# Two small moves in a planned schedule: a pair of VectorE transposes goes behind 35 filler units, and the bonus product changes its PSUM pool

## The chip, the core and the metric

The kernel runs on one core of one Trainium2 chip. The metric is device time in microseconds (us) of one execution, the median of several. Besides the times there is a profile of one further execution.

## The reference, cut to what matters

A decoder trunk of two layers works on 512 positions of width 1024 in float32. Each layer has three token mixers side by side (RWKV-7, retention, a spatial gating unit), gates that merge them, and a gated MLP. The change lies in the RWKV-7 mixer alone:

```python
def step(state, inp):
    r_t, w_t, k_t, v_t, kk_t, a_t = inp
    sa = jnp.einsum('bhvk,bhk->bhv', state, -kk_t)
    state = (state * w_t[:, :, None, :]
             + sa[..., None] * (kk_t * a_t)[:, :, None, :]
             + v_t[..., None] * k_t[:, :, None, :])
    y = jnp.einsum('bhvk,bhk->bhv', state, r_t)
    return state, y
...
y = y + jnp.sum(r * k * r_k, axis=-1, keepdims=True) * v
```

The last line is the bonus: for each head of 64 columns, the sum of r·k·r_k, times v.

## The kernel before, in words

**Order of the work.** Nearly all large products are float32 products made of three passes (`mm3`, lines 152 to 162): activations and weights are split into a high part and a low part, and line 156 issues three matmuls of 512 columns for each pair. Weights come in units of 128 rows by 512 columns. A unit is loaded by SyncE's queue (line 126), its high part is made by ScalarE (the cast of line 139, tiles `wh` or `sh`), its low part by VectorE (the subtraction of line 140, tiles `wl` or `sl`). One unit feeds 12 matmuls. `unit()` (lines 94 to 114) prepares units ahead of their use; in the stage of the change `AHEAD[None]` is 2, so that the call that hands out unit n has just emitted lines 139 and 140 of unit n + 2. The tags `wh` and `wl` have three buffers each.

**Who orders it.** Instructions are emitted in the order of the Python program. A scheduler then orders each engine's queue, by the order of emission, priorities and a simulated timeline; each engine works its queue off in order. `keep_in_program_order` (called `po`) fixes one instruction behind the instruction emitted just before it on the same engine; it adds no wait for another engine.

**RWKV-7 in chunks.** For each of four pairs of heads, `prep(m)` (lines 526 to 581) makes the decays and the scaled keys, and, in eight chunks of 64 positions, the products that the recurrence needs (lines 571 and 574), which ScalarE copies out of PSUM (lines 575 and 576). `bonus(m)` (lines 583 to 591) multiplies r·k·r_k by a block matrix of ones (lines 588 and 589), and VectorE multiplies the result by v (line 590). PSUM has eight banks: four of tag `acc`, taken by `acc()`, for the long accumulations of line 156, and four of tag `sm`, taken by `sm()`, for short products. `prep` takes six `sm` banks one after the other, and `bonus` takes a seventh.

**Solve.** Within a chunk a unit triangular system of 64 rows must be inverted for each head. `solve` (lines 756 to 821) inverts the blocks of 32 rows on VectorE, by a forward substitution of 31 dependent steps (lines 785 to 790), and joins the blocks on TensorE (lines 808 and 817). Between the two stand the first pair of 32 by 32 transposes, which makes `TD` (line 794), the second pair, which makes `TT` (line 797), and `diag(TT)`, four copies of diagonal blocks from `TT` into `G` (two on ScalarE, line 769, two on GpSimd, line 771). `then()` emits the turning of the scaled keys (lines 629 to 635): a VectorE transpose (line 631), a transfer out and eight transfers back on SyncE's queue. Line 808 reads `TD` and blocks of `G` that `diag` doesn't write; line 817 reads `TT`; the recurrence's loop (line 664) reads the diagonal blocks.

**Filler.** While VectorE substitutes, TensorE works on gate projections: `self.fill(n)` emits n steps of a generator, each one unit (`gates`, lines 433 to 448). Two steps make one accumulator, which VectorE takes out of PSUM (line 443). `FILL = (36, 2, 1)`: 36 steps go before line 808 is reached, two before line 817, one at each pause of the loop. In the profile's names `hi`, `lo` are the parts of the activations.

Of the kernel before, what the change touches and what calls it, by code (L numbers as in the profile page):

```python
# [23 lines left out]
FILL = (36, 2, 1)  # L24
# [27 lines left out]
class Emit:  # L52
# [408 lines left out]
    def rwkv(self, l, nst):  # L461
        nc, V, A, a = self.nc, self.nc.vector, self.nc.scalar, self.a
# [4 lines left out]
        po = self.tc.keep_in_program_order if l == 0 else lambda i: i  # L467
# [49 lines left out]
        hv, po = [slice(0, 64), slice(64, 128)], self.tc.keep_in_program_order  # L517
# [65 lines left out]
        def bonus(m):  # L583
            kp, r, v = kc[m], rc[m], Vf[m]
            V.scalar_tensor_tensor(kp, r, self.p("rk", m), kp, op0=MUL, op1=MUL)
            kh, kl = self.split(kp, self.r)
            pbn = self.sm()
            po(T.matmul(pbn, self.bonesR, kl, start=True, stop=False))
            po(T.matmul(pbn, self.bonesR, kh, start=False, stop=True))
            V.tensor_tensor(kp, v, pbn, op=MUL)  # L590
            bv.append(kp)
# [9 lines left out]
        prep(0)  # L601
        cols3(2)
        bonus(0)
        prep(1)
        cols3(3)
        bonus(1)
        prep(2)
        gd = col(13)
        bonus(2)
        prep(3)  # L610
        bonus(3)
# [144 lines left out]
    def solve(self, G, n2, then):  # L756


        V, A, T = self.nc.vector, self.nc.scalar, self.nc.tensor
        flat = lambda t: t.rearrange("p t s -> p (t s)")  # L760
        po = self.tc.keep_in_program_order
        grp = [slice(32 * i, 32 * i + 32) for i in range(4)]
        def diag(d):

            for i, R in enumerate(grp):
                g = G[R, :, 32 * (i % 2):32 * (i % 2) + 32]
                o, s = (d[R], g) if d is GD else (g, d[R])
                if i < 2:
                    A.copy(o, s)
                else:  # L770
                    self.nc.gpsimd.tensor_copy(o, s)
        GD = self.rw((128, 32, 32), "cs", 3)
        diag(GD)
        for h in range(2):
            self.nc.gpsimd.memset(G[64 * h + 32:64 * h + 64, :, 0:32], 0.0)
        NS = self.rw((128, 32, 32), "cs", 3)
        TS = self.rw((128, 32, 32), "cs", 3)
        TMP = self.rwp.tile([128, 288], F32, name=self.nm("TMP"))
        V.memset(TS, 0.0)
        V.memset(flat(TS)[:, 0:1024:33], 1.0)  # L780
        V.transpose(NS, GD.rearrange("p u t -> p t u"))
        nu = TMP[:, 256:288]
        V.transpose(nu, n2)
        V.tensor_tensor(NS, NS, nu.unsqueeze(1).to_broadcast([128, 32, 32]), op=MUL)
        for k in range(31):
            r, c = 31 - k, k + 1
            tmp = TMP[:, :r * c].rearrange("p (r c) -> p r c", c=c)
            V.tensor_tensor(tmp, NS[:, k + 1:, k:k + 1].to_broadcast([128, r, c]),
                            TS[:, k:k + 1, :c].to_broadcast([128, r, c]), op=MUL)
            V.tensor_tensor(TS[:, k + 1:, :c], TS[:, k + 1:, :c], tmp, op=ADD)  # L790
        V.tensor_tensor(TS, TS, nu.unsqueeze(2).to_broadcast([128, 32, 32]), op=MUL)
        TD = self.rw((128, 32, 32), "cs", 3)
        for e in (slice(0, 16), slice(16, 32)):
            V.transpose(TD[:, :, e].rearrange("p u s -> p s u"), TS[:, :, e].rearrange("p t s -> p s t"))
        TT = self.rw((128, 32, 32), "cs", 3)
        for e in (slice(0, 16), slice(16, 32)):
            V.transpose(TT[:, :, e].rearrange("p u t -> p t u"), TS[:, e])
        diag(TT)
        then()
        lo = [slice(64 * h, 64 * h + 32) for h in range(2)]  # L800
        hi = [slice(64 * h + 32, 64 * h + 64) for h in range(2)]
        self.fill(FILL[0])

        zs = [self.r((128, 16, 32), n="zs") for _ in range(2)]
        z = [[self.sm((128, 16, 32)) for _ in range(2)] for _ in range(2)]
        for g, i in [(g, i) for g in range(2) for i in range(16)]:
            for h in range(2):
                po(T.matmul(z[g][h][(hi, lo)[i % 2][h], i, :], G[lo[h], 16 * g + i, 32:64], TD[lo[h], 16 * g + i, :], start=True, stop=True))
        for g in range(2):
            for h in range(2):  # L810
                for e in range(2):
                    (V.tensor_copy if h else A.copy)(zs[g][hi[h], e::2], z[g][h][(hi, lo)[e][h], e::2])
        self.fill(FILL[1], True)
        pt = [[self.sm((128, 16, 32)) for _ in range(2)] for _ in range(2)]
        for g, i in [(g, i) for g in range(2) for i in range(16)]:
            for h in range(2):
                po(T.matmul(pt[g][h][(lo, hi)[i % 2][h], i, :], zs[g][hi[h], i, :], TT[hi[h], 16 * g + i, :], start=True, stop=True))
        for g in range(2):
            for h in range(2):
                for e in range(2):  # L820
                    (V.tensor_copy if h else A.copy)(G[lo[h], 16 * g + e:16 * g + 16:2, 32:64], pt[g][h][(lo, hi)[e][h], e::2])
# [620 lines left out]
```

## Time and profile before

| what | us |
|---|---|
| median of 3 runs | 1702.07 (1701.75 to 1702.5) |
| the profiled execution's own time | 1702.98 |
| its span | 1701.0 |
| TensorE busy | 1687.0 (99%) |
| VectorE busy | 1217.3 (72%) |
| ScalarE busy | 795.6 (47%) |
| GpSimd busy | 240.7 (14%) |

Layer 0's `solve` reaches line 808 at 200.9 us of the span, layer 1's at 1047.8 us. In a row of the timeline the first number is the start, the second the length, both in us; then come the engine (PE for TensorE, DVE for VectorE, ACT for ScalarE, POOL for GpSimd, SPq for SyncE's queue), the line, the operation, the tile written and the tiles read. A bracket at the end tells how long the engine stood idle before, and whose end released it.

### The profile page before, as it was taken

To read this page: it belongs to the slowest core of one execution; us is meant where nothing else is said; L and a number is where in the kernel's file an instruction comes from. 1 tells how busy PE (TensorE), PEld (TensorE's weight loads), DVE (VectorE), ACT (ScalarE), POOL (GpSimd) and SP (SyncE) were. 2 spreads that over 40 slices of the span, in tenths; PEclk is the share of its full clock that TensorE was granted. 3 is DMA by queue.
4 is the path that set the end of the run, shared out by engine and by line. 5 is a ranking of instruction groups with operands and counts; after the bars stand their busy time and mean duration, and the time that the engine had idled before them with its cause. 6 is when DMAs were issued, how large, how long until landed. Compare 5 with 4: busy or idle time off the path is not lost.

```text
span 1701.0 us, 27848 instructions
## 1 busy us (share of the span) xinstructions
PE 1687.0 (99%) x10214; PEld 1379.5 (81%) x10214; DVE 1217.3 (72%) x2113; ACT 795.6 (47%) x1367; POOL 240.7 (14%) x336
## 2 busy tenths in 40 slices
PE   9999999999999999999999999999999999999998
PEld 7888777888888888888888888777888888888886
DVE  6887745578669877655568887455786688887776
ACT  6563433554345444433346544435542544444565
POOL 2121000003301200003321210000132012220000
PEclk9999999999999999999999999999999999999999
DMA  5336553524544533147743265535254534443775
GB/s 179 90 106 196 176 179 103 174 93 161 192 144 147 193 124 99 63 143 264 242 150 97 93 206 182 178 101 180 87 163 166 153 96 142 143 141 115 244 242 168
DMA packets 147768, 260.01 MB, mean 153 GB/s; under 512 B 19600, under 2 KB 39952, under 8 KB 147632
## 3 DMA queue, kind: packets, MB, share of 16 engines
q1 hardware_dynamic: 122960, 192.87, 36.5%
q0 software_dynamic: 15888, 49.95, 8.8%
q10 hardware_dynamic: 8784, 15.42, 2.5%
q8 instruction: 80, 1.31, 0.3%
q14 instruction: 56, 0.46, 0.1%
HBM read 212.94 MB, written 45.22 MB: 152 GB/s over the span
## 4 chain that ended last, share of the span: by engine, by line
PE 90%; DMA 4%; DVE 3%; ACT 1%; issue 1%; SPq 1%; POOL 0%; ACTq 0%; DVEq 0%; POOLq 0%
PE acc L156 81%; PE sm L156 3%; PE sm L664 2%; DMA wr<-wall 2%; PE sm L917 1%; DVE wl L140 1%; PE sm L571 1%; DMA tr<-qkt 1%; DVE sl L140 0%; ACT wh L139 0%; PE sm L1022 0%; SPq L230 0%; ACT sh L139 0%; DMA x<-xT 0%; DMA bkS<-tr 0%
## 5 line engine op out<-in xcount | busy, mean ns | idle before, releaser
L156 PE MATMUL acc<-hi,sh 128*128 128x512 f32 x1108 | 431.9, 390 | 0.0
L156 PE MATMUL acc<-lo,sh 128*128 128x512 f32 x1108 | 431.6, 390 | 0.0
L156 PE MATMUL acc<-hi,sl 128*128 128x512 f32 x1108 | 424.5, 390 | 0.0
L139 ACT CAST sh<-wr 128x512 fp32r<-128x512 f32 (+1 forms) x375 | 226.7, 614 | 305.5 <-PE acc L156 166.9
L140 DVE TENSOR_TENSOR sl<-wr,sh 128x512 fp32r<-128x512 f32 (+1 forms) x375 | 253.5, 683 | 106.2 <-ACT sh L139 79.3
L140 DVE TENSOR_TENSOR wl<-wr,wh 128x512 fp32r<-128x512 f32 x238 | 168.5, 710 | 145.3 <-ACT wh L139 142.3
L139 ACT CAST wh<-wr 128x512 fp32r<-128x512 f32 x238 | 146.6, 619 | 241.2 <-PE acc L156 151.9
L156 PEld LDWEIGHTS acc<-lo,sh 128*128 128x128 f32 x1108 | 208.1, 188 | 43.8 <-issue 0.9
L156 PEld LDWEIGHTS acc<-hi,sl 128*128 128x128 f32 x1108 | 208.0, 188 | 43.5 <-DVE gth L1037 0.3
L156 PEld LDWEIGHTS acc<-hi,sh 128*128 128x128 f32 x1108 | 208.0, 188 | 43.3 <-issue 0.3
L156 PE MATMUL acc<-lo,wh 128*128 128x512 f32 x588 | 232.1, 395 | 1.5 <-DVE lo L215 1.1
L156 PE MATMUL acc<-hi,wl 128*128 128x512 f32 x588 | 230.3, 392 | 0.8 <-DVE wl L140 0.7
L156 PE MATMUL acc<-hi,wh 128*128 128x512 f32 x588 | 229.2, 390 | 0.0
L1088 ACT ACTIVATE cv<-fu,pc 128x512 f32<-128x512 f32 x88 | 71.7, 816 | 138.7 <-DVE fu L1086 138.6
L156 PEld LDWEIGHTS acc<-hi,wl 128*128 128x128 f32 x588 | 110.4, 188 | 27.2 <-DVE wl L140 3.4
L156 PEld LDWEIGHTS acc<-lo,wh 128*128 128x128 f32 x588 | 110.4, 188 | 26.7 <-DVE lo L215 1.8
L156 PEld LDWEIGHTS acc<-hi,wh 128*128 128x128 f32 x588 | 110.4, 188 | 22.1 <-issue 0.2
L156 PE MATMUL acc<-ah,sh 128*128 128x512 f32 x352 | 108.4, 389 | 0.0
L1089 DVE SCALAR_TENSOR_TENSOR cv<-fu,pc,cv 128x511 f32<-128x511 f32 x88 | 65.8, 749 | 34.5 <-ACT cv L1088 34.5
L156 PE MATMUL acc<-wl,hi 128*128 128x512 f32 x212 | 86.1, 406 | 0.0
L1086 DVE TENSOR_TENSOR fu<-acc,rsF 128x512 f32<-128x512 f32 x88 | 60.3, 685 | 31.9 <-PE acc L156 31.0
L156 PE MATMUL acc<-wh,hi 128*128 128x512 f32 x212 | 82.8, 391 | 0.0
(358 smaller groups left out, 2413.8 us busy)
## 6 DMA issues: line engine op xcount, KB each, us to landing
wr<-wall SPq DMA_DIRECT2D x488, 256.0 KB, 2.8
gd<-gth ACTq DMA_DIRECT2D x48, 256.0 KB, 3.2
gth<-gd POOLq DMA_DIRECT2D x48, 256.0 KB, 3.4
pre<-wdt POOLq DMA_DIRECT2D x44, 256.0 KB, 5.7
ts<-pre POOLq DMA_DIRECT2D x44, 256.0 KB, 2.8
wr<-ts SPq DMA_DIRECT2D x44, 256.0 KB, 3.9
wr<-wdn SPq DMA_DIRECT2D x40, 256.0 KB, 4.0
wr<-wdt SPq DMA_DIRECT2D x33, 256.0 KB, 3.6
```

The costliest lines, as they stand in the source:

```text
L139: self.kept(self.nc.scalar.copy(hi[:, :n], raw[:, :n]))
L140: self.kept(self.nc.vector.tensor_tensor(lo[:, :n], raw[:, :n], hi[:, :n], op=SUB))
L156: i = self.nc.tensor.matmul(*x, **y, **kw)
L571: i = T.matmul(pK[hv[1 - h], j, :], bk[hv[h], c, 1, :], x[hv[h], c, :], start=True, stop=True)
L664: po(T.matmul(o, l, r, start=start, stop=True, skip_group_check=True))
L917: po(T.matmul(X[h][:, i, :], lhsT, rhs, start=new[h], stop=stop, skip_group_check=True))
L1086: V.tensor_tensor(u, ps, self.rsF, op=MUL)
L1088: A.activation(t, u, AF.Identity, scale=self.p("cw2", j), bias=self.p("cb", j))
L1089: V.scalar_tensor_tensor(t[:, 1:], u[:, :511], self.p("cw1", j), t[:, 1:], op0=MUL, op1=ADD)
```

## The change

The second pair of transposes and `diag(TT)` are emitted behind 35 of the 36 filler steps, and each of the two transposes is kept behind what was emitted before it on VectorE. `then()` is now emitted ahead of them. The bonus product's bank comes from the four `acc` banks. No operation is added or taken away.

```diff
@@ -584,7 +584,7 @@
             kh, kl = self.split(kp, self.r)
-            pbn = self.sm()
+            pbn = self.acc()
             po(T.matmul(pbn, self.bonesR, kl, start=True, stop=False))
             po(T.matmul(pbn, self.bonesR, kh, start=False, stop=True))
             V.tensor_tensor(kp, v, pbn, op=MUL)
@@ -792,14 +792,15 @@
         TD = self.rw((128, 32, 32), "cs", 3)
         for e in (slice(0, 16), slice(16, 32)):
             V.transpose(TD[:, :, e].rearrange("p u s -> p s u"), TS[:, :, e].rearrange("p t s -> p s t"))
-        TT = self.rw((128, 32, 32), "cs", 3)
-        for e in (slice(0, 16), slice(16, 32)):
-            V.transpose(TT[:, :, e].rearrange("p u t -> p t u"), TS[:, e])
-        diag(TT)
         then()
         lo = [slice(64 * h, 64 * h + 32) for h in range(2)]
         hi = [slice(64 * h + 32, 64 * h + 64) for h in range(2)]
-        self.fill(FILL[0])
+        self.fill(FILL[0] - 1)
+        TT = self.rw((128, 32, 32), "cs", 3)
+        for e in (slice(0, 16), slice(16, 32)):
+            po(V.transpose(TT[:, :, e].rearrange("p u t -> p t u"), TS[:, e]))
+        diag(TT)
+        self.fill(1)
```

## The prediction

> **What bounds the kernel now.** I read the page first, then the list of who waits for whom with TensorE (PE) as the waiting engine, then the timeline of the stretches that this list points to.
>
> ```profile
> span 1701.0 us, 27848 instructions
> PE 1687.0 (99%) x10214; PEld 1379.5 (81%) x10214; DVE 1217.3 (72%) x2113; ACT 795.6 (47%) x1367; POOL 240.7 (14%) x336
> PE 90%; DMA 4%; DVE 3%; ACT 1%; issue 1%; SPq 1%; POOL 0%; ACTq 0%; DVEq 0%; POOLq 0%
> ```
>
> ```profile
> PE acc L156 <- DVE sl L140: 2.0, 6, 0.5
> PE acc L334 <- DVE rst L331: 1.5, 1, 1.5
> PE acc L156 <- DVE lo L215: 1.1, 2, 0.7
> PE acc L156 <- DVE wl L140: 0.7, 1, 0.7
> PE sm L664 <- DVE s L724: 0.4, 2, 0.2
> PE sm L588 <- ACT Y L576: 0.4, 1, 0.4
> PE acc L156 <- ACT wh L139: 0.3, 1, 0.3
> ```
>
> PE is busy for 99% of the span and makes 90% of the chain that ended last. The change removes no matmul, so only PE's pauses can shrink. All that the list names is 6.4 us. Two of its rows are what the change touches: 0.7 us, once, for a weight's low part from VectorE (line 140), and 0.4 us, once, for the bank of the bonus product (line 588, released by ScalarE's copy of line 576). No row shows PE waiting for an `acc` bank to be emptied (lines 443, 493). A fifth of a per cent of the time, about what a measurement of this kernel can tell from no change, is 3.4 us, over half of the list. The gain to be had is thus small from the outset.
>
> **The moved transposes, layer 0.** The first rows are PE's, then VectorE's and ScalarE's.
>
> ```profile
> 165.80 0.39 PE L156 MATMUL acc<-lo,wh 128*128 128x512 f32 x1
> 168.29 0.39 PE L156 MATMUL acc<-hi,wl 128*128 128x512 f32 x1
> ...
> 191.36 0.39 PE L156 MATMUL acc<-lo,wh 128*128 128x512 f32 x1
> 192.72 0.50 PE L156 MATMUL acc<-hi,wl 128*128 128x512 f32 x1 [0.74 <-DVE wl L140]
> 195.71 0.50 PE L156 MATMUL acc<-hi,wl 128*128 128x512 f32 x1
> 198.11 0.39 PE L156 MATMUL acc<-lo,wh 128*128 128x512 f32 x1
> ```
>
> ```profile
> 187.97 2.26 DVE L794 STREAM_TRANSPOSE cs<-cs 128x512 f32<-128x512 f32 x2
> 190.10 2.04 DVE L797 STREAM_TRANSPOSE cs<-cs 128x512 f32<-128x512 f32 x2
> 191.99 0.68 DVE L140 TENSOR_TENSOR wl<-wr,wh 128x512 fp32r<-128x512 f32 x1
> 194.96 0.69 DVE L140 TENSOR_TENSOR wl<-wr,wh 128x512 fp32r<-128x512 f32 x1 [1.70 <-ACT wh L139]
> 197.78 0.68 DVE L140 TENSOR_TENSOR wl<-wr,wh 128x512 fp32r<-128x512 f32 x1
> ```
>
> ```profile
> 188.58 0.63 ACT L139 CAST wh<-wr 128x512 fp32r<-128x512 f32 x1 [0.46 <-PE acc L156]
> 192.18 2.10 ACT L769 COPY GB<-cs 32x1024 f32<-32x1024 f32 x2 [2.97 <-DVE cs L797]
> 194.31 0.62 ACT L139 CAST wh<-wr 128x512 fp32r<-128x512 f32 x1
> ```
>
> The first two PE rows are the first and the last of a unit's 12 matmuls: 11 steps in 2.49 us, 0.226 us each. The unit that begins at 191.36 is the 34th filler unit. Its high part was ready at 189.2 (cast 188.58 + 0.63); its low part could have followed at 190.1, but stood in VectorE's queue behind the second pair of transposes until 191.99. PE waits. The pair does more: ScalarE, done with that cast at 189.2, has the `diag` copies next in its queue, stands idle 2.97 us until the pair is done, copies for 2.10 us, and only then casts the 35th unit (194.31), whose low part comes late as well (PE at 195.71). From 191.36 to 198.11 PE issues two units, 24 matmuls, in 6.75 us; at 0.226 they need 5.43. The pair costs 1.3 us here.
>
> Behind the change the pair stands behind line 140 of the 37th unit (the 35th call prepares two ahead), before the row at 197.78, the third line 140 behind the one at 191.99. That one needs the 34th unit's buffers, free at about 194.5 without the pause (191.36 + 12 x 0.226 + 0.39); cast and subtraction add 0.62 and 0.69, so the pair runs at about 196 to 198. VectorE waits for nothing new: line 794, at 187.97, comes behind the whole substitution. Queued behind the pair are line 140 of the 38th unit and line 443 of the 18th gate; behind ScalarE's copies, now at about 198 to 200.1, the casts of the 38th and 39th. Who waits for these:
>
> ```profile
> L808 PE MATMUL sm<-cs,GB x128: 191/191/212, 200.9 to 202.1; 32*32 32x32 f32 x128
> L817 PE MATMUL sm<-cs,zs x256: 184/191/212, 207.9 to 1056.0; 32*32 32x32 f32 x128
> 202.19 0.50 PE L156 MATMUL acc<-lo,wh 128*128 128x512 f32 x1
> ```
>
> The 37th unit starts at 202.19, the 38th a unit later at 204.9, and `TT` is first read at 207.9; with 1.3 us gained, 203.6 and 206.6. A line 140 that the pair holds until 198 is done by 198.7, and one whose cast waits for the copies until 200.1 by 201.4: 2 us early at the least. `diag` writes other blocks of `G` than line 808 reads, so line 808 doesn't wait for the copies. I take the whole 1.3 us as gained; the ends are a loss of 1.3 (the same pause at the new place, and in layer 1 as well) and a gain of 1.3.
>
> **The moved transposes, layer 1.**
>
> ```profile
> 1042.64 2.06 DVE L797 STREAM_TRANSPOSE cs<-cs 128x512 f32<-128x512 f32 x2
> 1044.53 0.69 DVE L140 TENSOR_TENSOR wl<-wr,wh 128x512 fp32r<-128x512 f32 x1
> 1045.41 0.40 PE L156 MATMUL acc<-hi,wl 128*128 128x512 f32 x1
> 1044.83 2.39 POOL L771 COPY GB<-cs 32x1024 f32<-32x1024 f32 x2 [53.62 <-DVE cs L797]
> ```
>
> The low part ends at 1045.22 and is read at 1045.41: 0.2 us to spare, no pause. There is nothing to gain here, and the pair, 2 us later, lands again before line 808 (1047.8), whose 1.3 us cover what it delays. Layer 1: 0.
>
> The rows at 1044.53 and 1044.83 also show a subtraction of two inputs beside GpSimd's copies: 0.69 us, as long as the one at 194.96, beside which GpSimd is idle. The Trainium skill says the opposite of what this would lead one to expect (GPSIMD Engine Reference, Specifications): GpSimd shares its SBUF interfaces with VectorE, and VectorE instructions with two SBUF inputs contend for them. By that rule the copies at their new place would lengthen the 38th unit's low part too; by the row they don't. In either case it has 2 us of cover; without cover a lengthening would be taken off the 1.3.
>
> **The bonus product's bank.** It is issued eight times; one of them pauses.
>
> ```profile
> 69.23 0.40 PE L156 MATMUL acc<-hi,wh 128*128 128x512 f32 x1
> 70.06 0.50 PE L588 MATMUL sm<-lo,bonesR 128*128 128x512 f32 x1 [0.43 <-ACT Y L576]
> 70.63 0.39 PE L156 MATMUL acc<-hi,wl 128*128 128x512 f32 x1
> 67.18 0.69 DVE L149 TENSOR_TENSOR lo<-rwc,hi 128x512 fp32r<-128x512 f32 x1
> ```
>
> Three matmuls (69.23 and the two of the bonus) take 1.40 us instead of 0.68: 0.72 us lost. Its operand was ready at 67.9 (67.18 + 0.69), so with an `acc` bank the product need not pause. It takes one `acc` bank of four for its two matmuls and the multiplication of line 590; the projections use one bank after the other for two units each, 24 x 0.226 = 5.4 us, so three give VectorE 10.8 us to empty one. And each `prep` gets an `sm` bank one product earlier.
>
> Does the 0.72 us reach the end? Not surely. PE meets a second bound:
>
> ```profile
> 168.56 0.69 DVE L140 TENSOR_TENSOR wl<-wr,wh 128x512 fp32r<-128x512 f32 x1 [0.95 <-ACT wh L139]
> 167.91 0.62 ACT L139 CAST wh<-wr 128x512 fp32r<-128x512 f32 x1 [2.20 <-DMA bkS<-tr]
> 180.48 0.39 PE L156 MATMUL acc<-lo,wh 128*128 128x512 f32 x1
> ```
>
> From 165.80 to 180.48 five units take 14.68 us where 13.58 would do: 1.1 us lost to weights whose cast waits, by the profile, for transfers of the key turning (`bkS`), which share SyncE's queue with the loads. If that queue keeps its times, a PE that comes 0.72 us earlier waits 0.72 us longer here, and the bonus gains 0. If the `prep`s and with them the turning come earlier too, the 0.72 stays, and at most the 1.1 us go as well. Ends 0 and 1.8; I take the middle of the first two, 0.4, since nothing in these rows tells the two apart.
>
> **Sum.** 1.3 + 0 + 0.4 = 1.7 us. The profiled execution took 1702.98 us by its own time, 0.9 above the median of the runs; from there 1701.3, from the median of 1702.07, which the forecast is for, 1700.4. Some of this may be paid back by an order that the scheduler chooses anew; I put 0.1 there: **1700.5 us**.
>
> **Rivals.** (A) *The pauses move instead of going*: the bonus is eaten at 165 to 180, and the pair delays a low part at its new place. For it speaks the 14.68 us stretch, against it the 2 us of cover. From a gain of 1 to a loss of 1.3: 1701.1 to 1703.4. A change that doesn't do what it says ends here too: if the scheduler put the 37th unit's line 140 early, the pair would stay where it is.
>
> (B) *Slower: the bonus product comes too early in PE's queue.* With its bank always free it is queued for when the simulated timeline has its operands, and these come from a ScalarE cast (line 148), which can stand behind a weight's cast that waits for its load:
>
> ```profile
> ACT wh L139 <- DMA wr<-wall: 58.6, 34, 5.7
> ```
>
> Such a wait is 1.7 us on average (58.6 / 34), 5.7 at most, and everything behind line 588 on PE waits along. One of eight products that meets it takes back the gain of 1.7; with three of eight the loss is 5.2 - 1.3 = 3.9 us, 1706.0, beyond a fifth of a per cent; it decides from there. Against it: the operand at 67.9 was ready 2.2 us before its product, and the product is kept behind the projections emitted before it.
>
> (C) *Faster than the sum*: all of 0.72 and 1.1 go as well, 1.3 + 1.8 = 3.1 us, 1699.0. It would need 0.3 us more to pass a fifth of a per cent.
>
> **Chances.** The forecast 0.50 (1699.9 to 1701.0), A 0.19, B 0.24 (of which I count 0.20 beyond 3.4 us), C 0.07 (0.04 beyond). So faster 0.04, same 0.76, slower 0.20. B's chance is more than its row alone would give, since it stands for the one way in which a new order of the queues could cost much. The range reaches from C, 1699.0, to B with three products, 1706.0.
>
> **What would show it.** Right: no pause of PE between the 34th and 36th filler unit of layer 0, line 797 at about 196 instead of 190.1 and behind three more lines 140, ScalarE's 2.97 us of idleness gone; line 588 into `acc` with no wait for line 576; the five units at 165 to 180 as slow as now or slower by up to 0.7 us. Wrong: PE waiting at line 588 for VectorE or ScalarE, a wait of line 156 for line 443 or 493 (`acc` too scarce), or new pauses on line 140 between 200 and 345 us or in layer 1.

## The result, and the profile after

| | before | changed |
|---|---|---|
| median of the runs, us | 1702.28 | 1756.48 |
| lowest to highest, us | 1701.75 to 1702.66 | 1752.78 to 1757.55 |
| profiled execution, us | 1702.98 | 1756.24 |
| its span, us | 1701.0 | 1754.5 |

The changed kernel is slower: its time is 1.031 times that of before (95% interval 1.0298 to 1.0322). The forecast was 1700.5, its range ended at 1706.0.

The page of the changed kernel, with its span, the engines' busy times and the chain that ended last:

```profile
span 1754.5 us, 27849 instructions
...
PE 1700.7 (97%) x10214; PEld 1386.3 (79%) x10214; DVE 1221.6 (70%) x2113; ACT 796.2 (45%) x1367; POOL 240.3 (14%) x336
...
PE 78%; DMA 6%; DVE 6%; issue 5%; ACT 3%; SPq 1%; POOL 0%; ACTq 0%; DVEq 0%; POOLq 0%
```

The span is 53.5 us longer. TensorE runs the same 10214 matmuls, is busy 13.7 us longer with them (1700.7 against 1687.0) and idle 39.8 us longer. PE's share of the chain falls from 90% to 78%: more of it now runs through VectorE, ScalarE and transfers. The longest rows of the list of who waits for whom, PE waiting (us in total, times, longest), name the places:

```profile
PE sm L571 <- DVE bk L563: 20.8, 4, 9.9
PE acc L588 <- DVE lo L149: 11.6, 4, 4.7
PE acc L156 <- ACT wh L139: 5.8, 4, 2.2
PE sm L533 <- ACT Y L576: 2.2, 2, 1.5
PE acc L156 <- DVE sl L140: 1.9, 4, 0.9
PE acc L334 <- DVE rst L331: 1.5, 1, 1.5
PE acc L156 <- DVE wl L140: 1.1, 2, 0.6
...
```

The two big rows are new. Both are in the preparation of the recurrence: line 571 is the first of a `prep`'s chunk products, line 588 is the bonus product, and what they wait for is their operand from VectorE. No row of the list has line 588 waiting for a bank, and none has line 156 waiting for an `acc` bank to be emptied. Now the stretches of the two preparations, first of the kernel before, then of the changed one (columns: stretch, its length, busy us and count of PE, PEld, DVE, ACT, POOL, then PEclk, the granted TensorE clock, the DMA share and GB/s):

```profile
60.00:130.00 70.00, 69.57 (x526) 56.72 (x525) 58.20 (x101) 43.38 (x74) 16.88 (x15) 1.00 0.30 92
920.00:1000.00 80.00, 80.00 (x518) 65.82 (x517) 66.23 (x111) 46.86 (x80) 17.23 (x16) 1.00 0.40 124
```

```profile
60.00:130.00 70.00, 54.23 (x442) 43.87 (x440) 58.92 (x94) 36.75 (x63) 21.81 (x20) 0.90 0.16 54
920.00:1000.00 80.00, 60.83 (x455) 48.76 (x454) 61.23 (x106) 42.17 (x74) 14.80 (x13) 0.87 0.18 56
```

Before, PE is busy there throughout. In the changed kernel it issues 84 and 63 matmuls fewer in the same time, is idle for 16 and 19 us, and has a granted clock of 0.90 and 0.87. PE's timeline of layer 0 shows the two kinds of pause:

```profile
88.02 0.39 PE L534 MATMUL sm<-hi,wus 128*128 128x512 f32 x1
91.97 0.79 PE L588 MATMUL acc<-lo,bonesR 128*128 128x512 f32 x1 [3.56 <-DVE lo L149]
92.56 0.63 PE L589 MATMUL acc<-hi,bonesR 128*128 128x512 f32 x1
92.99 0.63 PE L156 MATMUL acc<-lo,wh 128*128 128x512 f32 x1
...
104.63 0.39 PE L534 MATMUL sm<-hi,wus 128*128 128x512 f32 x1
114.88 0.44 PE L571 MATMUL sm<-X,bk 64*64 64x128 f32 x1 [9.87 <-DVE bk L563]
```

At 88.02 and at 104.63 PE has projections and filler left to run, and doesn't run them. Why is seen in the order of its queue. These are the places of the four bonus products of layer 0 (line 588) and of the first matmul of the first gate column, the filler, as the number of PE's matmuls in the trace that start ahead of each:

```
                          bonus 0  bonus 1  bonus 2  bonus 3   first gate
before                      341      478      616      755        502
changed                     332      476      568      636        638
```

Before, 119 more filler and projection matmuls stand ahead of the last bonus product. In the changed kernel the first gate comes right behind that product. In both kernels the accumulators in `acc` begin on PE in the order in which the program asks for them, as far as the trace tells them apart by their lines. The bonus products of `prep` 2 and 3 are asked for ahead of the filler; once they ask `acc`, the filler's accumulators stand behind them, and the bonus products can't run until the `prep` chain on VectorE and ScalarE has made their operand.

The price can be counted. These are the last bonus product and a later landmark of layer 0, before and then changed:

```profile
127.23 0.40 PE L589 MATMUL sm<-hi,bonesR 128*128 128x512 f32 x1
...
282.22 0.69 PE L664 MATMUL sm<-S,X 64*64 64x64 f32 x32 [0.22 <-DVE s L724]
```

```profile
119.08 0.40 PE L589 MATMUL acc<-hi,bonesR 128*128 128x512 f32 x1
...
144.53 0.50 PE L156 MATMUL acc<-lo,wh 128*128 128x512 f32 x1 [2.18 <-ACT wh L139]
...
149.43 0.50 PE L156 MATMUL acc<-lo,wh 128*128 128x512 f32 x1 [1.60 <-ACT wh L139]
...
304.93 0.69 PE L664 MATMUL sm<-S,X 64*64 64x64 f32 x32 [0.22 <-DVE s L724]
```

The product is reached 8.15 us sooner, but 119 matmuls of 0.227 us, 27.0 us of work, are still to be done. That leaves 18.9 us; two waits for weight casts, 2.18 and 1.60, make it 22.7. The landmark is late by 304.93 - 282.22 = 22.7. That the two agree so closely is in part luck: the changed kernel loses some 2 us more in small steps between 133 and 150 us (it is 24.9 us behind where the kernel before is at 127.00), and makes them up where the kernel before pauses, between 168 and 196 us. In layer 1 the same counting, with 146 matmuls, comes to 29 of the 30 to 31 us that this layer adds.

### The profile page after: what moved, and what is told of

It reads as the page before. It is cut to its first block, busy times and chain, and to the rows that moved or that the text cites. A ratio compares the mean times of both kernels' runs of the same rounds, so it can differ in the third digit from the quotient of the medians.

```text
span 1754.5 us, 27849 instructions
## 1 busy us (share of the span) xinstructions
PE 1700.7 (97%) x10214; PEld 1386.3 (79%) x10214; DVE 1221.6 (70%) x2113; ACT 796.2 (45%) x1367; POOL 240.3 (14%) x336
## 4 chain that ended last, share of the span: by engine, by line
PE 78%; DMA 6%; DVE 6%; issue 5%; ACT 3%; SPq 1%; POOL 0%; ACTq 0%; DVEq 0%; POOLq 0%
PE acc L156 70%; DMA wr<-wall 4%; PE sm L156 3%; PE sm L664 2%; DVE wl L140 1%; PE sm L918 1%; ACT wh L139 1%; DVE sl L140 1%; DMA wr<-wdt 1%; PE sm L571 1%; SPq L621 0%; DMA tr<-vT 0%; PE sm L1023 0%; ACT sh L139 0%; DMA tr<-qkt 0%
## 5 line engine op out<-in xcount | busy, mean ns | idle before, releaser
L156 PE MATMUL acc<-wh,lo 128*128 128x512 f32 x212 | 82.8, 390 | 0.0
```

The costliest lines, as they stand in the source:

```text
L156: i = self.nc.tensor.matmul(*x, **y, **kw)
```

## The experiments

Theory 1: the bonus product's place in `acc`'s queue of requests is what costs, since everything asked for behind it waits for the `prep` chain. Its rivals: the moved transposes with their pins cost the time; three banks are too few for columns and filler; the bonus product, pinned early in PE's queue, costs it by itself.

**The bonus's bank alone, and the transposes alone.** The first kernel is the one before with

```
-            pbn = self.sm()
+            pbn = self.acc()
```

> Only the bonus product's accumulator goes from sm to acc; the transposes stay as in the kernel before. Theory 1 (banks of acc are handed out in the order in which the program asks for them, so the bonus's request holds back the filler's accumulators until the prep chain has delivered its operand): about 1756 to 1758 us, TensorE idle at line 571 some 20 us in all and at line 588 some 11 us, as in the changed kernel. Rival (the transposes moved behind the filler, with their pins, cost the time): within 2 us of 1702.

The second is the changed kernel with `pbn = self.sm()`.

> Only the second pair of transposes and its copies move; the bonus product stays in sm. Theory 1: 1700 to 1702.5 us; the prediction's term for this part is 1.3 us less than before (1701.0), from layer 0 alone, no idle of TensorE at lines 571 and 588. Rival (the transposes cost the time): 1740 to 1756.

The bonus's bank alone: 1755.92 us, 1.0324 times before (1.0310 to 1.0338). The transposes alone: 1699.30 beside 1700.87 for the kernel before on the same chip, 0.9993 (0.9984 to 1.0002), which is between 2.7 us less and 0.3 us more. So the loss is the bank's. PE's waits with the bank alone have the two rows of the changed kernel again:

```profile
PE sm L571 <- DVE bk L563: 20.6, 3, 9.9
PE acc L588 <- DVE lo L149: 10.3, 4, 3.5
```

In the kernel with the transposes alone, the stretch that the prediction costed reads as follows; line 794 is the first pair of transposes, line 801 the moved one:

```profile
186.84 2.31 DVE L794 STREAM_TRANSPOSE cs<-cs 128x512 f32<-128x512 f32 x2
189.03 0.67 DVE L140 TENSOR_TENSOR wl<-wr,wh 128x512 fp32r<-128x512 f32 x1
...
190.19 0.70 DVE L140 TENSOR_TENSOR wl<-wr,wh 128x512 fp32r<-128x512 f32 x1
...
194.68 2.10 DVE L801 STREAM_TRANSPOSE cs<-cs 128x512 f32<-128x512 f32 x2
196.62 0.69 DVE L140 TENSOR_TENSOR wl<-wr,wh 128x512 fp32r<-128x512 f32 x1
196.81 2.11 ACT L769 COPY GB<-cs 32x1024 f32<-32x1024 f32 x2 [0.22 <-DVE cs L801]
```

The product that reads `TT`, by its line (shortest, median and longest in ns, first and last start):

```profile
L818 PE MATMUL sm<-cs,zs x256: 184/191/212, 205.8 to 1053.7; 32*32 32x32 f32 x128
```

A line 140 now follows the first pair at once, PE has no pause between 178 and 198 us, and ScalarE's idle time ahead of its copies is 0.22 us instead of 2.97. The product that reads `TT` begins at 205.8 instead of 207.9; 0.55 us of that lead was there already at the last bonus product.

**A guest with a ready operand.** Is it the bank, or what its holder waits for? The kernel with the transposes alone gets, ahead of each bonus product:

```
+            xa, dm = self.acc(), self.small((128, 8), "dm")
+            T.matmul(xa, self.bonesR, self.h[0][1], start=True, stop=False)
+            T.matmul(xa, self.bonesR, self.h[0][0], start=False, stop=True)
+            V.tensor_copy(dm, xa[:, 0:8])
```

> The bonus product stays in sm, but just ahead of each a pair of extra matmuls of the same shape takes a bank of acc, with operands that have long been ready (the bonus's weights and the first normed tile), unpinned, and VectorE reads 8 columns of it; nothing uses what it reads. So acc loses a bank as often as in the changed kernel, in the same place of the program, but nothing holds the request up. It adds 16 matmuls of about 0.23 us, 3.6 us, and 8 short VectorE instructions. Theory 1: 1703 to 1708 us. Rival (three banks are too few for the columns and the filler, whoever holds the fourth): 1740 to 1760, with TensorE idle at line 571 or at line 156 behind the reading of acc.

1716.54 us, 1.0093 (1.0077 to 1.0108). That is above what theory 1 gave by 8.5 us, and far below the rival's. Its list of PE's waits names neither line 571 nor a line 156 that waits for an `acc` bank; behind it is the row of the first preparation's stretch:

```profile
PE acc L156 <- DVE sl L140: 2.0, 3, 1.3
PE acc L156 <- ACT wh L139: 2.0, 3, 0.9
PE acc L334 <- DVE rst L331: 1.5, 1, 1.5
PE acc L156 <- DVE wl L140: 1.3, 3, 0.8
```

```profile
60.00:130.00 70.00, 69.75 (x526) 56.88 (x525) 58.03 (x103) 43.19 (x74) 16.45 (x15) 1.00 0.28 86
```

PE is busy for 69.75 of 70 us in the first preparation, which ends within 0.1 us of the kernel before. A fourth bank taken as often, at the same place, doesn't empty PE there. Some 12 us beyond the guest's own 3.6 come later: waits for the low parts of weights (line 140) at 330 to 350 us, for instance, 2.0 us where the kernel before has 0.6. Why the new order is worse there I did not settle.

**The filler asked for first.** The changed kernel, with

```
+        self.pool = None
+        self.fill(2)
+        self.pool = "p"
         bonus(2)
         prep(3)
+        self.pool = None
+        self.fill(6)
+        self.pool = "p"
         bonus(3)
...
-        self.fill(FILL[0] - 1)
+        self.fill(FILL[0] - 9)
```

> The changed kernel, bonus in acc, but two filler units are asked for ahead of the third bonus product and six ahead of the fourth; nine fewer follow in front of solve's products, so the filler as a whole is the same. Theory 1: the four gate accumulators are ahead of the bonus products in acc's queue and fill the gaps again: 1704 to 1720 us, the pauses of 9 to 10 us at line 571 in both layers gone, the 3.6 and 4.7 us at line 588 of the first bonus product still there. Rival (three banks are too few): 1740 or more. Rival (the bonus pair pinned too early in TensorE's queue costs the time by itself): no gain at line 588 and at most 5 us in all, so 1750 or more.

1722.05 us, 1.0124 (1.0109 to 1.0139): 33 of the 54 us come back, though the bonus is still in `acc`. (The filler ahead of `solve`'s products goes from 35 to 27 steps, eight fewer, not nine; the 36 steps in all are kept.) The row of line 571 waiting for VectorE is gone, the one of line 588 stays, as expected (3.5 us in layer 0, 3.4 and 2.3 in layer 1); the time is 2 us above what I gave.

```profile
PE acc L588 <- DVE lo L149: 9.3, 3, 3.5
```

**Which bonus products cost what.** The changed kernel with `pbn = self.acc() if m < 2 else self.sm()`, then with `m > 1`, then with `m == 0`.

> The changed kernel, but only the first two bonus products take their bank from acc; the third and fourth are back in sm. Theory 1 (a request that waits for the prep chain holds back the acc requests behind it): the two 9 to 10 us pauses at line 571 are gone, since the gate accumulators can start behind the second bonus; TensorE still waits at line 588 for the first bonus products, 3.6 and 4.7 us in the changed kernel's trace, and some 2 us for the second, and runs slowly for some us behind that. 1710 to 1722 us. Rival (acc has too few banks): between a third and two thirds of the loss without any particular place, 1720 to 1740.

> The mirror of the run before: only the third and fourth bonus products take acc. Theory 1: the pauses at line 571 stay, about 20 us in all, those at line 588 of the first bonus are gone: 1728 to 1742 us. The excess over the kernel before, added to that of the run with the first two, should give about the 54 us of the changed kernel.

> Only the first bonus product takes acc, which is the one whose 0.4 us wait for a bank of sm the change could remove. Theory 1: its wait for its own operand at line 588, 3.6 us in layer 0 and 4.7 us in layer 1 of the changed kernel, stays, with some us at a lower clock behind it: 1708 to 1716 us. The prediction's term would be 0.4 us less than the transposes alone, 1699.

The first two products in `acc`: 1724.42 us, 1.0126 (1.0111 to 1.0141). The last two: 1754.83, 1.0303 (1.0287 to 1.0319). The first alone: 1712.20, 1.0046 (1.0030 to 1.0063). The places are as theory 1 had them, with one exception: the 3.6 us pause of layer 0 (at 91.97 in the changed kernel) is the second bonus product's and not the first's, so that with the first alone line 588 waits once, 5.0 us, in layer 1. Two of the three times are not as given: 1724.42 is above theory 1's 1722 and by itself would fit its rival, 1754.83 is above 1742. The first two cost 21 us, the last two 52, and together they should have made 54. Here are the waits for the first two and then for the last two:

```profile
PE acc L588 <- DVE lo L149: 9.2, 3, 3.5
```

```profile
PE sm L571 <- DVE bk L563: 32.5, 4, 9.3
```

In the changed kernel lines 571 and 588 wait for 20.8 + 11.6 = 32.4 us. With the last two in `acc`, line 571 alone waits for 32.5. The two waits don't add up: the `prep` chain needs its time, and PE is idle for what it lacks in work until the chain ends, at whichever line it then stands. Work that may run ahead of the last bonus product sets that sum, and the last two products alone take all of it away: the last bonus product of layer 0 has 636 matmuls ahead of it in the changed kernel, with the bank alone and with the last two in `acc`, against 755 in the kernel before and 727 with the first two. Of the 21 us that the first two cost, line 588's waits are 9.2; where the rest arises was not followed.

**The filler held back without any bonus in `acc`.** The kernel with the transposes alone, with

```
-                pg = self.acc()
+                pg = self.sm() if br == 0 and m < 5 else self.acc()
```

in `gates`.

> No bonus product is in acc here: the kernel with only the transposes moved, in which the first five gate accumulators (the filler that TensorE runs in the gaps of the preps) are asked for from sm instead of acc. So acc has more free banks than in any other kernel, but the filler's requests stand in sm's queue behind those of all four preps. Theory 1 (it is the place in the queue of requests that counts): the same 9 to 10 us pauses at line 571 as with the third and fourth bonus in acc, and none at line 588 for the first bonus: 1728 to 1742 us, within 6 us of that run. Rival (acc is short of banks): about 1700, no pause at line 571.

1755.28 us, 1.0307 (1.0291 to 1.0323): like the run with the last two in `acc` it is above the 1742 given, and it is within 0.5 us of that run, with `acc` freer than ever. Its waits are those of that run, and its queue has the same order (341, 478, 566 and 636 matmuls ahead of the bonus products, 638 ahead of the first gate). First its waits, then the row of the first preparation's stretch:

```profile
PE sm L571 <- DVE bk L563: 33.3, 4, 9.3
...
PE sm L588 <- ACT Y L576: 0.7, 2, 0.5
```

```profile
60.00:130.00 70.00, 54.57 (x439) 44.56 (x438) 56.38 (x94) 37.35 (x63) 21.65 (x20) 0.88 0.17 54
```

So it is not `acc`, and not a lack of banks in it: it is filler whose request stands behind a request that the `prep` chain holds up. The gates now share the four `sm` banks, but their products wait little for one: the last row shown, 0.7 us, and 0.3 at line 533. Nor do the pins of the bonus product cost the time by themselves, since they are the same in the kernel before. Whether the loss would come without them isn't shown; no kernel without the pins was run.

No version beats both kernels by more than can be measured; the transposes alone are the nearest to it.

## Why the prediction was wrong

*The moved transposes: right.* Predicted were 1.3 us in layer 0, the pair at about 196 and ScalarE's idle time gone, and nothing in layer 1. Alone, the change puts the pair at 194.68, and the lead grows by 1.5 us in layer 0, from the last bonus product to the `TT` product, and by nothing at the same place of layer 1. By the times it is 1.6 us, with an interval that reaches past zero. VectorE's subtraction beside GpSimd's copies at the new place (196.62 in the fence above, while the copies run from 196.91 on) took 0.69 us: no lengthening, as in the row of layer 1. But neither row speaks against the rule quoted there, as the prediction had it: in both the subtraction began first, and the last section shows that this decides.

*The bonus's bank: wrong, and it is the step that failed.* "Ends 0 and 1.8" excluded a loss. The step behind it counted for how long a bank is held (three give VectorE 10.8 us) and looked for a wait on an emptied bank. That part holds: no such wait appeared in any kernel, and a guest with a ready operand left PE full in both preparations. What the step left out is the order of requests. In `sm` the bonus stood among the `prep`s' own products, which wait for the same chain anyway; in `acc` it stands ahead of the only work that PE can do meanwhile. The kernel before has PE at 69.57 of 70 us in a stretch where the chain on VectorE alone can't feed it (in the changed kernel PE is idle for 16 us there); I named no work that covers the chain there, nor asked what keeps that cover ahead of it. The term was a gain of 0.4 us; the bank by itself cost 55.0 (1755.92 - 1700.87).

The small gain didn't come either. The first product no longer pauses, but PE does, two matmuls earlier: line 533, which begins the next `prep`, now waits for ScalarE's copy of line 576, as the product did before. In the changed kernel:

```profile
67.36 0.50 PE L533 MATMUL sm<-lo,wus 128*128 128x512 f32 x1 [0.62 <-ACT Y L576]
...
67.93 0.40 PE L588 MATMUL acc<-lo,bonesR 128*128 128x512 f32 x1
```

The other kernels with the first bonus product in `acc` have this wait of 0.62 us too, and at 88 us the changed kernel is level with the kernel before. "The product need not pause" was true of the product and not of PE.

*Rival B named the right line and the wrong mechanism.* "PE waiting at line 588 for VectorE or ScalarE" is the second row of the waits, 11.6 us in four waits. I priced it at 1.7 us each, three of eight, from ScalarE's waits for a load. What is late is the subtraction of line 149, at the end of the `prep` chain, and the larger part of the loss isn't that wait but the filler that was no longer ahead. The range's upper end, 1706.0, came from that price.

*Rival A* had two halves. The pair's can be seen in the kernel with the transposes alone, where the pauses went and did not move. The bonus's came true at another place: its pause moved at once, to line 533, and not to 165 to 180 us.

## What to carry to other kernels

Before a tile is moved to another pool, ask not only whether the pool has a free buffer but who asks for one behind it: where buffers are given out in the order of the program, a request that hangs on a long chain is a barrier for everything behind it, filler above all. An engine that is busy for 99% owes that to work which floats over the chains of others; find out what lets it float, and count in the order of the queue how much stands ahead of each chain's end. Such idle times don't add up by place; what counts is the work that is left until the chain is done.

## What the runs showed of the hardware

*The clock.* Behind the 3.56 us pause at line 588, seven matmuls from 92.56 to 95.12 start 0.43 us apart, then they are 0.23 apart again. Behind the 9.87 us pause the 64 products of line 571 and its neighbour 574 start over 3.28 us (114.88 to 118.16); behind line 571's short pause of 0.19 us, at 99.85, they took 1.71. The granted clock of PE in two stretches of the changed kernel at that long pause (PE's busy time, PEclk, DMA share, GB/s), then in two behind a pause of 2.32 us that ends at 971.33:

```profile
110.00:115.00 5.00, 0.12 (x4) 0.50 0.00 2
115.00:120.00 5.00, 5.00 (x69) 0.59 0.15 56
```

```profile
972.00:974.00 2.00, 2.00 (x7) 0.60 0.00 0
974.00:976.00 2.00, 2.00 (x6) 0.55 0.00 0
```

It falls to 0.50 during the long pause and is still low for some us behind it. The Trainium skill has the rule (TensorE: Matmul & The Clock Gate, Part 1: The HAM clock gate): a window of about 3.4 us without work halves the clock, and about as long of steady work brings it back. The 3.56 us pause and the slow starts until 95.12 agree with it. But the length of a pause alone doesn't decide: behind the pause of 2.32 us matmuls are slow from 972.77 to 975.33, and in the kernel with the filler asked for first, pauses of 3.43 and 2.32 us (ending at 927.31 and 949.82) have no slow matmul behind them. In the whole changed kernel 26 slow matmuls of 512 columns make 5.2 us, part of the 13.7 us by which PE is busy longer.

*VectorE beside GpSimd.* The chain that the bonus product at 91.97 waits for ran slower than before; on VectorE a weight's low part (line 140) and the product's own (line 149) were longer than usual. VectorE's rows of the changed kernel, with GpSimd's selections, then one subtraction with GpSimd's copies:

```profile
86.91 2.36 POOL L579 TENSOR_SCALAR_AFFINE_SELECT Y<-Y 64x1024 f32<-64x1024 f32 x2 [11.81 <-ACT Y L576]
...
88.14 1.67 DVE L140 TENSOR_TENSOR wl<-wr,wh 128x512 fp32r<-128x512 f32 x1
...
89.34 2.04 POOL L580 TENSOR_SCALAR_AFFINE_SELECT GB<-GB 64x512 f32<-64x512 f32 x2
...
90.78 1.13 DVE L149 TENSOR_TENSOR lo<-rwc,hi 128x512 fp32r<-128x512 f32 x1
```

```profile
123.01 2.48 POOL L771 COPY cs<-GB 32x1024 f32<-32x1024 f32 x2
123.06 1.53 DVE L140 TENSOR_TENSOR wl<-wr,wh 128x512 fp32r<-128x512 f32 x1
```

Lines 140 and 149, two inputs from SBUF each, took 1.67, 1.13 and 1.53 us; alone they take 0.68 to 0.69. What decides is not whether GpSimd selects or copies but who begins first. In the traces of the kernel before, the changed one and the one with the transposes alone, 13 such subtractions began ahead of an instruction of lines 579, 580 or 771 that started during them: they took 0.65 to 0.72 us. Another 26 began while one of these had at least 0.18 us still to run: they took 0.72 to 1.67 us, and each ended 0.53 to 0.55 us behind the end of that instruction. The Trainium skill's rule on the shared interfaces (GPSIMD Engine Reference, Specifications) thus holds for the subtraction that begins second. Beside GpSimd's fills of line 775, which read no tile, it wasn't longer (0.68 us at 1005.67, with 0.45 us of a fill to run); why not, no run here shows.
